# Two layers of a diffusion backbone: the gating and the second products of the expert passes, each moved a turn later

## The chip, the cores and the metric

One NeuronCore of one Trainium2 chip runs the whole program in one launch. The metric is the device time in microseconds (us), the median of several executions. Beside it stands one profiled execution, from which all rows below are taken. TensorE multiplies, VectorE, ScalarE and GpSimd work on elements, and SyncE issues the DMA transfers. Each engine runs its own instructions in order.

## The reference

Two layers work on 256 latent and 256 context tokens of width 1024. Layer 0 is a mixer of short convolution and attention, layer 1 a bidirectional RWKV-7 mixer, and each is followed by a PEER expert network: for each token and each of 8 heads the best 16 of 16384 single-neuron experts are chosen through product keys, and

```python
gate = jax.nn.softmax(top_s, axis=-1)
u = u_tab[idx]
v = v_tab[idx]
act = jax.nn.gelu(jnp.einsum('nd,nhkd->nhk', xc, u, preferred_element_type=jnp.float32), approximate=False)
return jnp.einsum('nhk,nhkd->nd', (gate * act).astype(v.dtype), v)
```

In layer 0 this network runs for the latent and for the context tokens, in layer 1 for the latent tokens only. All in float32.

## The kernel before

**The passes.** The expert network is not gathered but computed densely: a pass takes 256 tokens through all 16384 experts, in 128 blocks of 128 experts, one block E in each turn of the loop in `Peer.run` (L1166). A turn has these parts. `first(E)` (L1111) makes 24 matmuls of U with the tokens, 8 slices in three terms (high by high, low by high, high by low), into a PSUM tile H, and ScalarE applies GELU to H in place (L1120). `gate(E)` (L1123) multiplies H on VectorE with the block's gates G (L1127), zero for tokens that did not choose the expert, and splits the result into a high part `gwh` (ScalarE) and a low part `gwl` (VectorE). `second(E)` (L1133) makes 12 matmuls of 512 columns that add V times gates to four PSUM accumulators. `prep_u` and `prep_v` split the loaded U and V rows into high and low parts: `uh` and `vh` on ScalarE, `ul` half on VectorE and half on GpSimd, `vl` on GpSimd (on VectorE in every other turn of the first 32). `load_u` and `load_v` issue the 512 KB loads on the sync queue.

**The gates.** `gen(gq, j)` (L1019) prepares the gates of 32 blocks ahead, 16 tokens at a time, in every second turn: VectorE makes a one-hot `oh` of the low index, a one-hot `eq` of the high index and two products `A` of it with the gate's high and low part; 32 small matmuls (16 in layer 1) put them together in PSUM, and ScalarE copies them to G (in layer 1 VectorE adds the low parts).

**The order in a turn.** Source order in turn E: `first(E)`, `gate(E)`, `gen`, `second(E-1)`, `prep_v(E)`, load of V, `prep_u(E+1)`, `load_u(E+2)` and the store `keep_u`. At the turn between passes `second(E-1)`, the end of the pass and the split of the new tokens come first. The first 32 blocks of a `Peer` have their first products made ahead, so turns 0 to 31 have none. The tile framework places waits and may reorder instructions within an engine.

**Three passes.** The first `Peer` object runs two passes of layer 0 with the same U and V; in the first, low parts of U are stored to DRAM (`keep_u`) and in the second loaded back (`ul<-low`). The second `Peer` runs the pass of layer 1.

**The shadow.** Beside the two passes of layer 0 other work runs in four slots of every turn: the key scores and choices for the second pass, layer 1's modulation, and `rwkv_ctx` (L1999), the whole RWKV mixer of the context. These are generators that `beside` (L235) advances so that each is done on schedule: `rwkv_ctx` with NCTX = 530 units between turns 132 and 253. A `yield` names how many units the piece before it took. In its scan, `step` (L477) of one head pair makes a right side, its product (UV, copied by ScalarE and VectorE at L512), the state's update (L518) and pauses between them; `woven` sets the steps of one head pair beside the preparation of the next, with the factor `pace` on the pauses. The shadow's matmuls share four PSUM tiles (`mm`) with H and with the gates' products.

Of the kernel before, what the change touches and what calls it, by code (L numbers as in the profile page):

```python
# [253 lines left out]
class Scan:  # L254
# [222 lines left out]
    def step(self, i, S0, last=False):  # L477

        k, st, kn, pl = self.k, self.st, self.kn, self.ql
        V, S, T = k.V, k.S, k.T  # L480
        cs = (i, 3 - i)
        N = 128 * kn
        heads = [(d, j, hh, R2[hh]) for d in range(2) for j in range(kn) for hh in range(2)]

        def at(p, d, j, r):
            o = 64 * (kn * d + j)
            return p[r, o:o + 64]

        def f4(p):
            return p[:, :N].rearrange("p (d k n) -> p d k n", d=2, k=kn)  # L490

        def tile(name):
            return pl.tile([128, 2, kn, 64], F32, name=name, bufs=2 if name == "state" else None)

        rhs = self.ps()
        for d, j, hh, r in heads:
            T.matmul(at(rhs, d, j, r), lhsT=self.tri(d, hh, j, cs[d], 0)[self.fresh], rhs=self.UV[d][self.fresh, cs[d], j, hh],
                     start=d + j == 0, stop=S0 is None and d + j == kn)
        if S0 is not None:
            for d, j, hh, r in heads:  # L500
                T.matmul(at(rhs, d, j, r), lhsT=self.zop(d, hh, j, cs[d], 0), rhs=S0[r, d, j], start=False, stop=d + j == kn)
        yield from self.apart()
        rsb = self.right_side(f4(rhs))
        yield 0.5 if self.lean else None
        pu = self.ps()
        for d, j, hh, r in heads:
            T.matmul(at(pu, d, j, r), lhsT=self.rop(d, hh, 4 * j + cs[d]), rhs=rsb(d, hh, j), start=True, stop=True)
        yield from self.apart()
        for d in range(2):
            for hh in range(2):  # L510
                e = S.copy if hh == 0 else V.tensor_copy
                e(self.UV[d][R2[0], cs[d], :, hh], pu[R2[hh], 64 * kn * d:64 * kn * (d + 1)].rearrange("p (k n) -> p k n", k=kn))  # L512
        yield 0.5 if self.lean else None
        Sn = None
        if not last:
            pS = self.ps()
            for d, j, hh, r in heads:
                T.matmul(at(pS, d, j, r), lhsT=self.tok[d][:, j, cs[d], 64 * hh:64 * hh + 64], rhs=self.UV[d][:, cs[d], j, hh],  # L518
                         start=True, stop=True)
            yield from self.apart()  # L520
            Sn = tile("state")
            src = f4(pS)
            if S0 is not None:
                ts = Sn
                V.tensor_add(ts, S0, src)
                src = ts
            V.tensor_tensor(Sn, src, self.PC[:, i, :, :, None].to_broadcast([128, 2, kn, 64]), ALU.mult)
        if st:
            if i == 0:
                self.y = pl.tile([128, 4, kn, 64], F32, name="y", bufs=1)  # L530
            py = self.ps()
            for d, j, hh, r in heads:
                T.matmul(at(py, d, j, r), lhsT=self.zop(d, hh, j, cs[d], 1), rhs=S0[r, d, j], start=d + j == 0, stop=False)
            for d, j, hh, r in heads:
                T.matmul(at(py, d, j, r), lhsT=self.tri(d, hh, j, cs[d], 1), rhs=self.UV[d][:, cs[d], j, hh], start=False, stop=d + j == kn)
            y = self.y
            yi = (y[:, 0::3], y[:, 1:3], y[:, 2:0:-1], y[:, 3::-3])[i]
            if i < 2:
                S.copy(yi, f4(py))
            else:  # L540
                V.tensor_add(yi, yi, f4(py))
        yield 0.5 if self.lean else None
        return Sn

    def readout(self):
# [324 lines left out]
class Peer:  # L870
# [147 lines left out]

    def gen(self, gq, j):  # L1019

        n, q = divmod(gq, 4)
        pl, V = self.pl, self.k.V
        i16, g16 = self.IT[n]
# [14 lines left out]
        V.tensor_tensor(eq, self.iotaR[:, None, 32 * q:32 * q + 32].to_broadcast(sh), per_token(i16[:, 0]).to_broadcast(sh), ALU.is_equal)  # L1038
        for i in range(2):
            V.tensor_tensor(A[:, i], eq, per_token(g16[:, i]).to_broadcast(sh), ALU.mult)  # L1040
        G = self.GT[gq]
        if gq == 0 or self.shadow:
            p = self.k.mm() if gq else self.k.acc()
            for m in range(16):
# [16 lines left out]
    def load_u(self, E):  # L1061
        if E < self.NT:
            n, e = divmod(E, 128)
            ur = self.pu.tile([128, D], F32, name="raw", bufs=4)
            self.k.Y.dma_start(ur, self.k.I["peer_u"][self.passes[n][0], e])
            ul = None
            if self.again(n):
                ul = self.pu.tile([128, 8, 128], F32R, name="ul", bufs=2)
                self.k.Y.dma_start(ul.rearrange("p t i -> p (t i)").bitcast(F32), self.LOW[e])
            self.U[E] = ur, ul  # L1070

    def again(self, n):

# [49 lines left out]
    def gate(self, E):  # L1123
# [1 line left out]
        W = self.W[E]  # L1125
        W2 = self.k.mm()[:, :256] if E < LOOK else W
        self.k.V.tensor_mul(W2, W, self.GT[E // 32][:, E % 32])  # L1127
        wh = pl.tile([128, 256], F32R, name="gwh", bufs=2)
        wl = pl.tile([128, 256], F32R, name="gwl", bufs=2)
        self.k.split(wh, wl, W2)  # L1130
        self.W[E] = (wh, wl)

    def second(self, E, slot=lambda: None):  # L1133
# [11 lines left out]
                slot()  # L1145
        if e == 127:
            self.finish(n)

    def finish(self, n):
        k = self.k  # L1150
# [13 lines left out]
        self.load_v(E + 2)  # L1164

    def run(self):  # L1166
        NT, NP = self.NT, len(self.passes)
        self.load_v(1)
        for E in range(NT + 1):
            if E == LOOK:  # L1170
                self.ew.close()
            slot = (lambda: self.shadow(E)) if self.shadow and LOOK <= E < NT else (lambda: None)
            turn = E % 128 == 0 and 0 < E
            if E % 128 == 125:
                self.near(E // 128)
            if turn:
                self.last(E - 1, slot)
                if E < NT:
                    self.load_x(E // 128)
                self.en.close()  # L1180
            if LOOK <= E < NT:
                self.first(E, slot)
            if E < NT:
                self.gate(E)
                gq = E // 32 + 1
                if gq < 4 * NP and E % 2 == 0:
                    if gq % 4 == 0 and E % 32 == 0:
                        self.begin(gq // 4)
                    self.gen(gq, (E % 32) // 2)
            slot()  # L1190
            if E > 0 and not turn:
                self.last(E - 1, slot)
            else:
                slot()
            if LOOK <= E + 1 <= NT:
                self.prep_u(E + 1)
                if LOOK <= E:
                    self.load_u(E + 2)
            slot()
            if LOOK <= E + 1 < NT:  # L1200
                self.keep_u(E + 1, self.U[E + 1][1])
        self.es.close()
        self.er.close()


class K:
# [792 lines left out]
    def rwkv_ctx(self, hd, dr, sS, lean=True):  # L1999
# [3 lines left out]
        with tc.tile_pool(name="sU", bufs=1, reuse_waits="tile") as U, tc.tile_pool(name="sA", bufs=1, reuse_waits="tile") as A, tc.tile_pool(name="sP", bufs=1, reuse_waits="tile") as tp:  # L2003
# [37 lines left out]
            yield from prepare(0)  # L2041
            for g in range(8):
                yield from sc.rows()
                yield from woven(chunks(sc.twin(), g, 1.7 if g < 7 else 1.0), prepare(g + 1) if g < 7 else iter(()))

    def mixer1_tensors(self):
        dp = self.dp
# [236 lines left out]
```

## Time and profile before

| | us |
|---|---|
| median of 3 runs | 3877.7 |
| lowest and highest | 3869.63 and 3879.46 |
| the profiled execution | 3874.92 |
| its span, first to last instruction | 3873.1 |
| passes of layer 0, first second product to end | about 506 to 2483 |
| pass of layer 1, second products | about 3176 to 3867 |

Over the span TensorE is busy 90%, VectorE 65%, ScalarE 45%, GpSimd 46%, and the mean granted TensorE clock is 0.942. The layer 0 passes end in two places: the first at about 1394 us, the second at about 2483 us. Busy TensorE time includes matmuls at half clock, so busy time and granted clock are read together.

### The profile page before, as it was taken

How to read it: one execution, taken by the hardware profiler on the slowest of the kernel's cores; microseconds unless marked ns; L12 is line 12 of the kernel's file. 1: busy time of each engine (PE TensorE's matmuls, PEld its weight loads, DVE VectorE, ACT ScalarE, POOL GpSimd, SP SyncE). 2: the span in 40 equal slices, each digit the busy share in tenths (PEclk: the TensorE clock that was granted, in tenths of full speed). 3: DMA queues.
4: the chain of work that ended last, by engine and by line, in shares of the span. 5: the costliest groups of instructions: out<-in, count | busy, mean ns of one | idle time of the engine just before them, and what ended most of it. 6: DMA issues, size and time to landing. Idle time of an engine off the chain costs nothing.

```text
span 3873.1 us, 73036 instructions
## 1 busy us (share of the span) xinstructions
PE 3482.2 (90%) x29031; PEld 3035.8 (78%) x29031; DVE 2503.7 (65%) x5274; ACT 1726.0 (45%) x2815; POOL 1798.4 (46%) x1000
## 2 busy tenths in 40 slices
PE   7998889998899899998999999886787778999999
PEld 6678778997787688987877777785676776899998
DVE  3569897658954466446766655478877889655622
ACT  3343455554443355554444444453223344555544
POOL 1122545665454544443333333434434443677776
PEclk9999899999899999999999999897898889999999
DMA  7373656776588777764555555541024234555554
GB/s 241 113 241 130 213 175 216 256 244 214 193 298 287 255 275 250 249 220 169 189 186 180 190 200 186 179 150 25 17 73 136 90 108 142 169 179 180 178 186 155
DMA packets 337535, 710.51 MB, mean 183 GB/s; under 512 B 41220, under 2 KB 199560, under 8 KB 336168
## 3 DMA queue, kind: packets, MB, share of 16 engines
q1 hardware_dynamic: 337192, 705.84, 55.0%
q8 instruction: 227, 3.72, 0.4%
q14 instruction: 116, 0.95, 0.1%
HBM read 624.45 MB, written 81.30 MB: 182 GB/s over the span
## 4 chain that ended last, share of the span: by engine, by line
PE 35%; DVE 14%; issue 2%; POOL 2%; ACT 2%; DMA 0%; DVEq 0%; POOLq 0%; ACTq 0%; SPq 0%
PE acc L1142 12%; PE mm L1247 6%; PE mm L1248 5%; PE mm L1249 5%; DVE A L1040 1%; DVE prod L465 1%; PE mm L727 1%; DVE TT L468 1%; PE mm L851 1%; DVE oh L1034 1%; DVE zz L654 1%; DVE vl L1243 1%; DVE mm L1127 1%; DVE wz L841 0%; PE mm L518 0%
## 5 line engine op out<-in xcount | busy, mean ns | idle before, releaser
L1243 POOL TENSOR_TENSOR vl<-raw,vh 128x1024 fp32r<-128x1024 f32 x352 | 902.5, 2564 | 949.7 <-ACT vh L1242 893.0
L1247 PE MATMUL mm<-xh,uh 128*128 128x256 f32 x3072 | 899.6, 293 | 30.2 <-ACT uh L1096 29.7
L1248 PE MATMUL mm<-xh,ul 128*128 128x256 f32 x3072 | 891.5, 290 | 22.6 <-DVE ul L1101 16.1
L1249 PE MATMUL mm<-xl,uh 128*128 128x256 f32 x3072 | 885.5, 288 | 0.0
L1101 POOL TENSOR_TENSOR ul<-raw,uh 128x512 fp32r<-128x512 f32 x320 | 503.0, 1582 | 388.6 <-ACT uh L1096 358.5
L1247 PEld LDWEIGHTS mm<-xh,uh 128*128 128x128 f32 x3072 | 604.0, 197 | 56.5 <-ACT uh L1096 34.6
L1248 PEld LDWEIGHTS mm<-xh,ul 128*128 128x128 f32 x3072 | 605.2, 197 | 39.8 <-DVE ul L1101 20.8
L1249 PEld LDWEIGHTS mm<-xl,uh 128*128 128x128 f32 x3072 | 605.2, 197 | 16.2 <-issue 15.7
L1127 DVE TENSOR_TENSOR mm<-mm,G 128x256 f32<-128x256 f32 x320 | 137.1, 429 | 645.7 <-ACT mm L1120 645.0
L1142 PE MATMUL acc<-vh,gwh 128*128 128x512 f32 x1536 | 517.8, 418 | 39.6 <-ACT gwh L1242 37.0
L1242 ACT CAST vh<-raw 128x1024 fp32r<-128x1024 f32 x384 | 403.0, 1049 | 296.8 <-issue 167.2
L1142 PE MATMUL acc<-vh,gwl 128*128 128x512 f32 x1536 | 499.9, 407 | 17.2 <-DVE gwl L1243 16.0
L1142 PE MATMUL acc<-vl,gwh 128*128 128x512 f32 x1536 | 494.4, 403 | 13.4 <-DVE vl L1243 11.9
L1096 ACT CAST uh<-raw 128x1024 fp32r<-128x1024 f32 x384 | 400.1, 1042 | 14.5 <-DMA raw<-in_peer_u_dram 14.3
L1120 ACT ACTIVATE mm<-mm 128x256 f32<-128x256 f32 x320 | 117.9, 368 | 596.7 <-PE mm L1249 595.8
L1142 PEld LDWEIGHTS acc<-vh,gwl 128*128 128x128 f32 x1536 | 293.5, 194 | 98.8 <-DVE gwl L1243 34.5
L1142 PEld LDWEIGHTS acc<-vl,gwh 128*128 128x128 f32 x1536 | 296.7, 194 | 85.1 <-DVE vl L1243 15.1
L1142 PEld LDWEIGHTS acc<-vh,gwh 128*128 128x128 f32 x1536 | 268.2, 195 | 88.5 <-ACT gwh L1242 41.5
L1034 DVE TENSOR_TENSOR oh<-iotaR,i 128x2048 f16<-128x2048 f16 x192 | 268.4, 1398 | 19.6 <-ACT i L949 19.6
L1040 DVE TENSOR_TENSOR A<-eq,g 128x512 f16<-128x512 f16 x384 | 222.3, 610 | 53.2 <-PE mm L1047 25.0
L1101 DVE TENSOR_TENSOR ul<-raw,uh 128x512 fp32r<-128x512 f32 x192 | 192.9, 1005 | 61.4 <-ACT uh L1096 61.3
L1242 ACT CAST gwh<-mm 128x256 fp32r<-128x256 f32 x384 | 143.9, 375 | 173.0 <-DVE mm L1127 172.4
(421 smaller groups left out, 6148.0 us busy)
## 6 DMA issues: line engine op xcount, KB each, us to landing
raw<-in_peer_u_dram SPq DMA_DIRECT2D x384, 512.0 KB
raw<-in_peer_v_dram SPq DMA_DIRECT2D x384, 512.0 KB
low<-ul SPq DMA_DIRECT2D x128, 512.0 KB
ul<-low SPq DMA_DIRECT2D x128, 512.0 KB
wraw<-in_ada_w_dram SPq DMA_DIRECT2D x48, 1024.0 KB
wraw<-in_peer_wq_dram SPq DMA_DIRECT2D x16, 1024.0 KB
wraw<-in_ev_w_in_dram SPq DMA_DIRECT2D x9, 1024.0 KB
wraw<-in_ev_w_out_dram SPq DMA_DIRECT2D x8, 1024.0 KB
```

Source lines behind the costliest of these rows:

```text
L1034: V.tensor_tensor(oh, self.iotaR[:, None].to_broadcast([128, 8, 128, 2]), per_token(i16[:, 1]).to_broadcast([128, 8, 128, 2]), ALU.is_equal)
L1040: V.tensor_tensor(A[:, i], eq, per_token(g16[:, i]).to_broadcast(sh), ALU.mult)
L1096: k.S.copy(uh, ur)
L1101: (le or (k.V, k.P)[i]).tensor_sub(ul[:, t], ur[:, t], uh[:, t].bitcast(F32))
L1120: self.k.S.activation(W, H, AF.Gelu)
L1127: self.k.V.tensor_mul(W2, W, self.GT[E // 32][:, E % 32])
L1142: self.k.T.matmul(self.ACC[n][2 * tb + dh], lhsT=a[:, 128 * tb:128 * tb + 128], rhs=b[:, 512 * dh:512 * dh + 512], start=e == 0 and a is w ...
L1242: self.last_copy = self.S.copy(hi, src).ins
L1243: (le or self.V).tensor_sub(lo, src, hi.bitcast(F32))
L1247: self.T.matmul(out, lhsT=ah, rhs=bh, start=start, stop=False)
L1248: self.T.matmul(out, lhsT=al, rhs=bh, start=False, stop=False)
L1249: self.T.matmul(out, lhsT=ah, rhs=bl, start=False, stop=stop)
```

## The change

In `Peer.run`, turn E now begins with `gate(E-1)`, then loads the tokens at a turn between passes, prepares the low part of U for the next turn and issues the raw load of U for E+2, makes the one-hots (`spread`, the first half of `gen`), then `first(E)`, the load of a kept low part (`load_low`), then `second(E-2)` with `prep_v(E-1)` and the load of V, then the gates' products (`gather`, the second half of `gen`), and the store. The loop has two turns more. `gwh` and `gwl` get a third buffer. In the lean scan's `step` three pauses of 0.5 become 1.0, and the pace 1.7 becomes 1.4.

```diff
@@ Scan.step (three places)
-        yield 0.5 if self.lean else None
+        yield 1.0 if self.lean else None
@@ Peer.gen is cut in two
+        self.spread(gq, j)
+        self.gather(gq, j)
+    def spread(self, gq, j):
...
+        self.hot = oh, A
+    def gather(self, gq, j):
+        V, G, s, (oh, A) = self.k.V, self.GT[gq], slice(16 * j, 16 * j + 16), self.hot
@@ Peer.load_u
-            ul = None
-            if self.again(n):
-                ul = self.pu.tile([128, 8, 128], F32R, name="ul", bufs=2)
-                self.k.Y.dma_start(ul.rearrange("p t i -> p (t i)").bitcast(F32), self.LOW[e])
-            self.U[E] = ur, ul
+            self.U[E] = ur, None
+    def load_low(self, E):
+        n, e = divmod(E, 128)
+        if E < self.NT and self.again(n):
+            ul = self.pu.tile([128, 8, 128], F32R, name="ul", bufs=2)
+            self.k.Y.dma_start(ul.rearrange("p t i -> p (t i)").bitcast(F32), self.LOW[e])
+            self.U[E] = self.U[E][0], ul
@@ Peer.gate
-        wh = pl.tile([128, 256], F32R, name="gwh", bufs=2)
-        wl = pl.tile([128, 256], F32R, name="gwl", bufs=2)
+        wh = pl.tile([128, 256], F32R, name="gwh", bufs=3)
+        wl = pl.tile([128, 256], F32R, name="gwl", bufs=3)
@@ Peer.run, the loop after
+        for E in range(NT + 2):
+            slot = (lambda: self.shadow(E)) if self.shadow and LOOK <= E < NT else (lambda: None)
+            if 0 < E <= NT:
+                self.gate(E - 1)
             if E == LOOK:
                 self.ew.close()
+            if E < NT and E % 128 == 125:
                 self.near(E // 128)
+            if E < NT and E % 128 == 0 and E:
+                self.load_x(E // 128)
+            if LOOK <= E + 1 < NT:
                 self.prep_u(E + 1)
                 if LOOK <= E:
                     self.load_u(E + 2)
+            gq = E // 32 + 1
+            due = gq < 4 * NP and E % 2 == 0
+            if due:
+                if gq % 4 == 0 and E % 32 == 0:
+                    self.begin(gq // 4)
+                self.spread(gq, (E % 32) // 2)
+            if LOOK <= E < NT:
+                self.first(E, slot)
+                self.load_low(E + 2)
             slot()
+            if E > 1:
+                self.last(E - 2, slot)
+            if due:
+                self.gather(gq, (E % 32) // 2)
             if LOOK <= E + 1 < NT:
                 self.keep_u(E + 1, self.U[E + 1][1])
+            slot()
@@ rwkv_ctx
-                yield from woven(chunks(sc.twin(), g, 1.7 if g < 7 else 1.0), prepare(g + 1) if g < 7 else iter(()))
+                yield from woven(chunks(sc.twin(), g, 1.4 if g < 7 else 1.0), prepare(g + 1) if g < 7 else iter(()))
```

`finish`, which ends a pass, now also closes the pool of the pass's last rows (in `second`), as `run` did before.

## Rows read from the trace of the kernel before

**Rows 1.** By stage: stretch, length, busy PE, PEld, DVE, ACT, POOL; clock, DMA, GB/s
```profile
620.00:1000.00 380.00, 358.64 (x2967) 327.24 (x2962) 261.61 (x638) 184.99 (x269) 220.49 (x107) 0.97 0.71 236
1000.00:1390.00 390.00, 350.35 (x2875) 286.50 (x2875) 229.18 (x437) 165.06 (x252) 193.63 (x94) 0.96 0.77 264
1390.00:1800.00 410.00, 386.85 (x3281) 349.47 (x3281) 216.45 (x400) 210.34 (x345) 180.60 (x107) 0.97 0.70 238
1800.00:2483.00 683.00, 635.83 (x5625) 540.80 (x5624) 399.12 (x853) 306.69 (x532) 241.45 (x127) 0.95 0.56 188
3176.00:3300.00 124.00, 103.47 (x622) 77.43 (x621) 120.44 (x175) 57.19 (x95) 44.80 (x18) 0.94 0.41 136
3300.00:3865.00 565.00, 565.00 (x3991) 514.00 (x3991) 279.66 (x479) 286.61 (x448) 420.62 (x190) 1.00 0.55 176
```

**Rows 2.** Waits of TensorE, 620 to 2483 us: total us, times, longest
```profile
PE mm L518 <- DVE UV L512: 38.4, 21, 4.0
PE acc L1142 <- ACT gwh L1242: 30.8, 17, 3.8
PE mm L1248 <- DVE ul L1101: 16.1, 13, 4.6
PE acc L1142 <- DVE gwl L1243: 10.9, 11, 3.8
PE mm L667 <- DVE bk L633: 8.3, 4, 4.2
...
PE mm L518 <- ACT UV L512: 3.5, 5, 1.1
PE mm L1247 <- ACT uh L1096: 3.4, 4, 2.2
PE mm L1047 <- DVE A L1040: 3.2, 1, 3.2
PE acc L1142 <- ACT vh L1242: 2.6, 1, 2.6
```

**Rows 3.** Waits of TensorE, 1000 to 1390 us
```profile
PE mm L1248 <- DVE ul L1101: 15.4, 12, 4.6
```

**Rows 4.** Waits of VectorE and of ScalarE, 506 to 2483 us
```profile
DVE mm L1127 <- ACT mm L1120: 389.9, 117, 7.6
ACT gwh L1242 <- DVE mm L1127: 163.8, 76, 6.9
```

**Rows 5.** Busy time around one gap of TensorE, at the end of a pass
```profile
1384.00:1388.10 4.10, 1.52 (x7) 0.93 (x5) 2.92 (x5) 3.26 (x6) 0.00 (x0) 0.95 0.79 282
1388.10:1394.30 6.20, 5.81 (x13) 4.13 (x14) 2.87 (x4) 2.09 (x2) 3.64 (x2) 0.50 0.97 363
1394.30:1403.80 9.50, 9.50 (x94) 8.95 (x93) 6.66 (x11) 4.74 (x8) 4.48 (x3) 0.99 0.85 306
```

**Rows 6.** Timeline of one turn, VectorE and GpSimd: start us, length us, engine, line
```profile
3607.37 1.20 DVE L1034 TENSOR_TENSOR oh<-iotaR,i 128x2048 f16<-128x2048 f16 x1
3608.50 2.62 DVE L1038 TENSOR_TENSOR eq<-iotaR,i 128x512 f16<-128x512 f16 x1
...
3611.39 1.52 DVE L1101 TENSOR_TENSOR ul<-raw,uh 128x512 fp32r<-128x512 f32 x1
...
3607.52 3.33 POOL L1243 TENSOR_TENSOR vl<-raw,vh 128x1024 fp32r<-128x1024 f32 x1 [0.53 <-DVE G L1059]
```

**Rows 7.** Timeline of VectorE in one step of the scan
```profile
2113.83 0.23 DVE L512 COPY UV<-mm 64x64 f32<-64x64 f32 x1
2113.97 1.03 DVE L474 STREAM_TRANSPOSE X<-TT 128x512 f32<-128x512 f32 x1
...
2115.52 0.19 DVE L512 COPY UV<-mm 64x64 f32<-64x64 f32 x1
```

**Rows 8.** Timeline of ScalarE in one turn
```profile
1492.19 1.03 ACT L1096 CAST uh<-raw 128x1024 fp32r<-128x1024 f32 x1
...
1494.33 0.37 ACT L1242 CAST gwh<-mm 128x256 fp32r<-128x256 f32 x1
```

More of the change, by code (lines that the diff above doesn't have):

```diff
@@ L512, in step @@
                 e(self.UV[d][R2[0], cs[d], :, hh], pu[R2[hh], 64 * kn * d:64 * kn * (d + 1)].rearrange("p (k n) -> p k n", k=kn))
-        yield 0.5 if self.lean else None
+        yield 1.0 if self.lean else None
         Sn = None
@@ L541, in step @@
                 V.tensor_add(yi, yi, f4(py))
-        yield 0.5 if self.lean else None
+        yield 1.0 if self.lean else None
         return Sn
@@ L1040, in gen @@
             V.tensor_tensor(A[:, i], eq, per_token(g16[:, i]).to_broadcast(sh), ALU.mult)
-        G = self.GT[gq]
+        self.hot = oh, A
+    def gather(self, gq, j):
+        V, G, s, (oh, A) = self.k.V, self.GT[gq], slice(16 * j, 16 * j + 16), self.hot
         if gq == 0 or self.shadow:
@@ L1147, in second @@
             self.finish(n)
+            self.en.close()
     def finish(self, n):
@@ L1168, in run @@
         self.load_v(1)
-        for E in range(NT + 1):
+        for E in range(NT + 2):
+            slot = (lambda: self.shadow(E)) if self.shadow and LOOK <= E < NT else (lambda: None)
+            if 0 < E <= NT:
+                self.gate(E - 1)
             if E == LOOK:
                 self.ew.close()
-            slot = (lambda: self.shadow(E)) if self.shadow and LOOK <= E < NT else (lambda: None)
-            turn = E % 128 == 0 and 0 < E
-            if E % 128 == 125:
+            if E < NT and E % 128 == 125:
                 self.near(E // 128)
[L1176 to L1195, printed above, removed]
+            if E < NT and E % 128 == 0 and E:
+                self.load_x(E // 128)
+            if LOOK <= E + 1 < NT:
                 self.prep_u(E + 1)
```

## The prediction

> **What bounds the kernel now.** I read the stages first: one row of busy time for each stretch, cut where the turns change character [rows 1]. A turn handles one block E of 128 experts: 24 first products, a GELU, a gating, 12 second products. From 3300 to 3865 us TensorE is busy for 565.00 of 565 us at granted clock 1.00: 96 turns of 5.9 us with no gap, so no reordering can shorten them. From 3176 to 3300 us (turns 0 to 31 of the last pass, which have no first products) VectorE is busy 120.44 of 124 us and sets the pace. The two passes of layer 0 are the open part. In the four stretches from 620 to 2483 us TensorE is idle for 21.4 + 39.6 + 23.1 + 47.2 = 131.3 us, while no other engine is over 70% busy; there the turns also carry shadow work of other stages.
>
> Second, who ended these idle times [rows 2]. The rows shown make 117.2 of the 131.3 us: second products waiting for gates or V parts (gwh 30.8, gwl 10.9, vh 2.6, together 44.3), first products waiting for U parts (ul 16.1, uh 3.4, together 19.5, of which 15.4 lie between 1000 and 1390 us [rows 3]), gates' products waiting for A (3.2), and 41.9 us in a shadow, the scan's state product L518 waiting for its UV copies. That last wait is nearly all of the idle time after 1800 us.
>
> Third, why the gates are late [rows 4]. VectorE stood still 389.9 us, 117 times, in front of the gating product L1127 because the GELU of the same turn was not done, 3.3 us each time, with everything behind it on VectorE standing too; ScalarE stood 163.8 us in front of gwh for that same product. Gate and second product are links of a chain inside one turn.
>
> Fourth, the price of a gap beyond its own length [rows 5]. From 1384.0 to 1388.1 us TensorE worked 1.52 us of 4.1. The 13 matmuls behind it ran at granted clock 0.50 and filled 6.2 us; then 0.99 came back. The gap cost about as much again as it lasted. A granted clock of 0.97, 0.96, 0.97 and 0.95 in the four stretches [rows 1], taken as work lost, is 11.4 + 15.6 + 12.3 + 34.2 = 73.5 us.
>
> **The gating, a turn later.** gate(E-1) opens turn E: one VectorE product, one ScalarE copy, one VectorE subtraction, none new. Its GELU ended a turn earlier, so VectorE no longer stops for it, and the second products that need these gates come in turn E+1, over 5 us on. All of the 44.3 us has its cause removed; what was queued behind the blocked product (one-hots, low parts, the shadow's copies) is freed also. A wait on ScalarE stays: the GELU still sits in its queue and waits for TensorE, with shadow copies behind it.
>
> **The low part and load of U.** prep_u(E+1) (uh on ScalarE, halves of ul on VectorE and GpSimd) moves from the end of turn E to its head, so first(E+1) has a whole turn of cover. 19.5 us is open to this. On the sync queue the load of raw for E+2 moves to the head with it, before the V load and before what the shadow issues; its lead to its cast stays one turn. The load of a kept low part now comes behind first(E), which frees its buffer, and is needed in turn E+2. The store of a low part stays at the end, when it has long been ready, so it stops holding the queue. If cover is gone anywhere, it is DMA: between 1000 and 1390 us the engines are 0.77 busy, and in the gap rows 0.79 and 0.97 [rows 1, 5]. A transfer that is late stays late, so I cut the first three classes (44.3 + 19.5 + 3.2 = 67) by a quarter: 50 us gained, bounds 30 and 67.
>
> **One-hots first, gates' products last.** No instruction is added: four VectorE operations go to the head, 32 (later 16) small matmuls and the copy to the end. The 3.2 us for A is counted above. What this adds: in every second turn the head holds gating, a low half, oh, eq and two A in one block of VectorE. Its operations stretch beside GpSimd: eq took 2.62 us at 3608.50 while GpSimd's vl ran for 3.33 us from 3607.52 [rows 6]. oh, eq and a low half make 1.20 + 2.62 + 1.52 = 5.3 us in these rows; with gating and A I estimate the block at 4 us where nothing stretches and 8 where all does. The shadow's VectorE copies of the first slot stand behind it. Also the first product now sits in its PSUM buffer (one of four shared with the shadow) until the next turn's gating rather than for a few us. The trace of before has neither state. Nearest row: the shadow waits that are not for gates, bk with 8.3 us [rows 2]; and the UV class with 41.9 us is what such queueing costs when it is bad. I charge 30 us with their clock, nearer to the small class; bounds 0 and 85, the two classes doubled by half again for the clock.
>
> The Trainium skill, "SBUF — State Buffer", section "SBUF: two separate sides", says that VectorE and GpSimd share one port pair as a lock, the loser standing for the other's whole instruction. The eq row agrees: it ended at 3611.1 with vl's end at 3610.9. By that rule the head's one-hots would meet only a low half on GpSimd instead of vl, and in the pass with kept low parts nothing; the charge would be near 0 and the sum 107 us, 3768 us, which lies on the side of rival (a).
>
> **Shadow steps.** The lean scan's three pauses of 0.5 become 1.0 and the pace 1.7 becomes 1.4. The space between the UV copies and L518 goes from 0.85 to 1.4 units, where a slot gets 530/(4 x 121) = 1.1 units; so the two never share a slot. Not all is cured: at 2113.83 and 2115.52 us the two halves of a UV copy are parted by a transpose of 1.03 us and another in VectorE's own queue [rows 7]. I take half, 20 us; bounds 0 and 42. The length: per head group 4 x 4.5 x 1.7 = 30.6 units become 4 x 6 x 1.4 = 33.6, both below the 37.5 units of the preparation woven beside it, so only the last group grows, 18 to 24 units of 530, some 1.4 turns, hidden while the scan still ends before turn 253 (my count is about 522 of 530).
>
> **Clock.** Before 1800 us the gained 50 is 60% of the 84 us idle, and I take 60% of 39.3: 23 us. After it 20 of 47.2 us goes: 42% of 34.2, 14 us. Bounds 0 and 73.
>
> **Ends and edges.** Two turns more in the loop, without work of their own; the second products are the same number. At the turn between passes the x split now stands straight before first(128) and the old gap [rows 5] goes: 0, bounds -6 and +6. Turns 0 to 31 are VectorE's: 0, bounds -4 and +4 [rows 1]. The deeper gwh and gwl buffers cost nothing in time.
>
> **Sum.** 50 + 20 + 23 + 14 - 30 = 77, say 75 us, against the profiled execution of 3874.9 us (1.8 us around its span): 3800 us. The median of the runs, 3877.7, lies 2.8 us above that execution; I do not correct for it.
>
> **The rivals.** (a) More comes back: the classes go whole, 67 + 42, with their share of the clock (109/131 of 73.5, 61), less 30: 3735 us. For it: gaps and slow clock go together in the rows. (b) The shadow takes most of it: TensorE runs in order, shorter turns leave the shadow's copies less time, and UV-like waits grow. Gates gain 50 + 23, no gain in the scan, charge 50: about 3850 us. (c) The order in the text is not the order on the engines: at 1492.19 us ScalarE ran uh, which the text puts last in the turn, ahead of gwh at 1494.33 us [rows 8]; if the builder already sorts by readiness, little moves: 3875 us. Against it: 389.9 us of blocked gating product shows that the sorting does not reach over turns. (d) Slower: the block at the turn's head. With 96 one-hot turns in the shadowed part, the 107 us of gains are used up when TensorE waits 1.1 us longer in each; at 1.4 us it is 134 us, 27 us over: 3902 us. For it: a block of 4 to 8 us, against some 1.5 us between two slots (5.9 us by four). Against it: before, the same block stood in the middle of the turn, with a 3.3 us stop in front of it [rows 4].
>
> **How the numbers follow.** Forecast (3770 to 3830) 0.48; (a) 0.17; (b) 0.16; (c) 0.08; (d) 0.11. A measurement of this kernel tells about 0.3%, 12 us, from no change. Forecast, (a) and (b) are faster: 0.81; (c) is the same: 0.08; (d) is slower: 0.11. The range leaves out (d), most of (c) and the far end of (a): 3725 to 3870.
>
> **What the profile after would show.** L1127 no longer waits for L1120; L1142 hardly waits for gwh and gwl, L1248 not for ul; TensorE's idle time from 620 to the end of layer 0's passes near 75 us and the granted clock there near 0.98; the two passes some 75 us shorter in all; L518's waits about halved. The last 96 turns stay 565 us. The forecast is wrong if new waits of shadow matmuls for VectorE or for a PSUM buffer come in their place, or if V or U casts wait for DMA between 1000 and 1390 us.

## The result and the profile after

The changed kernel takes 3811.79 us (median; 3805.39 to 3815.91), the kernel before 3875.26 us in the same session: a ratio of 0.9842, with a 95% interval from 0.9823 to 0.9861, or 63.5 us less. The forecast was 3800 us. Its profiled execution took 3805.39 us, 69.5 us less than that of before.

To see where these 69.5 us lie I cut both traces at the first matmul of the same blocks, so that a stretch is the same work in every kernel. Blocks 0 to 127 are the first pass of layer 0, 128 to 255 the second, 256 to 383 the pass of layer 1. Each row below is the difference of two start times in one profiled execution, in us. Beside before and after stand the four runs that answer most; they come below.

| from first product to first product | before | after | e1 order only | e2 steps only | e7 low part last | e8 gating in turn |
|---|---|---|---|---|---|---|
| start to block 32 (with turns 0–31) | 616.3 | 610.9 | 615.7 | 614.6 | 611.8 | 615.2 |
| 32 to 64 | 254.7 | 252.0 | 256.6 | 254.1 | 252.8 | 253.7 |
| 64 to 96 | 249.7 | 250.7 | 249.4 | 247.8 | 250.5 | 248.9 |
| 96 to 127 | 259.0 | 233.7 | 232.9 | 259.9 | 264.7 | 233.9 |
| 127 to 132, end of a pass | 37.6 | 44.5 | 42.4 | 37.9 | 39.3 | 44.1 |
| 132 to 160 | 231.6 | 230.7 | 230.4 | 231.7 | 228.1 | 232.2 |
| 160 to 255, the scan beside it | 825.9 | 798.3 | 807.5 | 800.5 | 808.3 | 806.5 |
| layer 1's mixer, to block 287 | 699.1 | 696.3 | 696.0 | 693.7 | 696.3 | 695.9 |
| 287 to 288: turns 0–31, last pass | 130.7 | 115.0 | 115.8 | 130.6 | 116.0 | 127.6 |
| 288 to the last second product | 561.2 | 564.4 | 564.4 | 561.2 | 564.4 | 561.6 |

Three rows carry the gain: 25.3, 27.6 and 15.7 us. One row costs: the end of the pass, 6.9 us. The mixer row, where the kernels do not differ, scatters from 693.7 to 702.3 us over all runs below, so a difference of some 8 us in one row of one profile proves little by itself.

The stages of the kernel after; the columns are those of [rows 1].

```profile
620.00:1000.00 380.00, 360.10 (x3012) 326.71 (x3011) 266.01 (x670) 189.64 (x271) 217.80 (x107) 0.98 0.71 237
1000.00:1390.00 390.00, 360.58 (x3046) 300.47 (x3045) 227.17 (x424) 172.69 (x264) 202.56 (x98) 0.96 0.81 283
1390.00:1800.00 410.00, 387.06 (x3321) 348.60 (x3320) 246.76 (x422) 218.13 (x355) 186.78 (x108) 0.97 0.69 230
1800.00:2431.00 631.00, 593.06 (x5396) 509.92 (x5395) 393.55 (x809) 292.42 (x508) 233.33 (x120) 0.97 0.58 198
3117.00:3232.00 115.00, 100.48 (x643) 77.81 (x641) 112.44 (x175) 60.00 (x100) 47.63 (x19) 0.96 0.46 152
3232.00:3786.00 554.00, 554.00 (x3936) 499.66 (x3937) 291.15 (x478) 285.60 (x444) 382.62 (x188) 1.00 0.55 179
```

In the first four rows TensorE is idle 19.9 + 29.4 + 22.9 + 37.9 = 110 us, where it was 131.3; the clock's share, worked out as in the prediction, is 7.6 + 15.6 + 12.3 + 18.9 = 54 us, where it was 73.5. The last row is full at clock 1.00 as before.

TensorE's waits after, 620 to 2431 us: total us, times, longest. They answer to [rows 2].

```profile
PE mm L1260 <- DVE ul L1112: 24.1, 15, 3.1
PE mm L518 <- DVE UV L512: 13.6, 14, 2.3
PE mm L501 <- DVE state L527: 11.3, 5, 3.6
...
PE mm L507 <- DVE rsb L742: 4.6, 2, 2.3
PE mm L727 <- DVE R L720: 4.6, 5, 1.9
PE mm L727 <- DVE t L697: 4.3, 1, 4.3
```

The waits for `gwh` and `gwl` (30.8 and 10.9 us) are gone. `ul` (L1112, L1101 before) is now the largest with 24.1 us. Of the shadow's waits, L507 and L727 are new, and L501 has grown from 1.0 us. All but 0.6 us of the waits for `ul` lie between blocks 64 and 96 (862.8 to 1113.5 us):

```profile
PE mm L1260 <- DVE ul L1112: 23.5, 14, 3.1
```

### The profile page after: what moved, and what is told of

It is laid out like the page before. It is cut to its first block, busy times and chain, and to the rows that moved or that the text cites. A ratio compares the mean times of both kernels' runs of the same rounds, so it can differ in the third digit from the quotient of the medians.

```text
span 3803.6 us, 73097 instructions
## 1 busy us (share of the span) xinstructions
PE 3438.2 (90%) x29031; PEld 3003.0 (79%) x29031; DVE 2532.4 (67%) x5274; ACT 1737.4 (46%) x2817; POOL 1772.1 (47%) x1000
## 5 line engine op out<-in xcount | busy, mean ns | idle before, releaser
L1255 POOL TENSOR_TENSOR vl<-raw,vh 128x1024 fp32r<-128x1024 f32 x352 | 879.5, 2499 | 856.8 <-ACT vh L1254 776.4
L1259 PE MATMUL mm<-xh,uh 128*128 128x256 f32 x3072 | 909.2, 296 | 36.0 <-ACT uh L1107 32.6
L1260 PE MATMUL mm<-xh,ul 128*128 128x256 f32 x3072 | 897.4, 292 | 36.8 <-DVE ul L1112 24.1
L1112 POOL TENSOR_TENSOR ul<-raw,uh 128x512 fp32r<-128x512 f32 x320 | 497.5, 1565 | 484.6 <-ACT uh L1107 433.4
L1153 PE MATMUL acc<-vh,gwh 128*128 128x512 f32 x1536 | 503.1, 408 | 11.2 <-ACT gwh L1254 9.1
L1153 PE MATMUL acc<-vh,gwl 128*128 128x512 f32 x1536 | 485.9, 397 | 4.8 <-DVE gwl L1255 4.5
L1153 PE MATMUL acc<-vl,gwh 128*128 128x512 f32 x1536 | 483.6, 396 | 4.2 <-POOL vl L1255 4.1
L1045 DVE TENSOR_TENSOR A<-eq,g 128x512 f16<-128x512 f16 x384 | 331.7, 890 | 116.5 <-PE mm L1055 64.7
L1153 PEld LDWEIGHTS acc<-vh,gwh 128*128 128x128 f32 x1536 | 264.8, 192 | 56.2 <-ACT gwh L1254 10.9
L1039 DVE TENSOR_TENSOR oh<-iotaR,i 128x2048 f16<-128x2048 f16 x192 | 254.3, 1324 | 21.6 <-ACT i L949 19.5
L1112 DVE TENSOR_TENSOR ul<-raw,uh 128x512 fp32r<-128x512 f32 x192 | 186.3, 970 | 86.6 <-ACT uh L1107 86.4
```

The source lines that it names most:

```text
L1039: V.tensor_tensor(oh, self.iotaR[:, None].to_broadcast([128, 8, 128, 2]), per_token(i16[:, 1]).to_broadcast([128, 8, 128, 2]), ALU.is_equal)
L1112: (le or (k.V, k.P)[i]).tensor_sub(ul[:, t], ur[:, t], uh[:, t].bitcast(F32))
L1153: self.k.T.matmul(self.ACC[n][2 * tb + dh], lhsT=a[:, 128 * tb:128 * tb + 128], rhs=b[:, 512 * dh:512 * dh + 512], start=e == 0 and a is w ...
L1255: (le or self.V).tensor_sub(lo, src, hi.bitcast(F32))
L1259: self.T.matmul(out, lhsT=ah, rhs=bh, start=start, stop=False)
L1260: self.T.matmul(out, lhsT=al, rhs=bh, start=False, stop=False)
```

## Experiments

Theory: the reordering gains because the links inside a turn (gating before second product, low part before first product) lose their waits; the steps gain in the scan. Rivals: one of the two does it all; and in turns 0 to 31 the cause is the meeting of VectorE and GpSimd.

**Order and steps apart (e1, e2).** e1 is the kernel after with the old steps, e2 the kernel before with the new ones. The edit of e1, which stands in three places of `step` for the first line (that of e2 is its reverse on the kernel before):

```diff
-        yield 1.0 if self.lean else None
+        yield 0.5 if self.lean else None
...
-                yield from woven(chunks(sc.twin(), g, 1.4 if g < 7 else 1.0), prepare(g + 1) if g < 7 else iter(()))
+                yield from woven(chunks(sc.twin(), g, 1.7 if g < 7 else 1.0), prepare(g + 1) if g < 7 else iter(()))
```

> The changed kernel with the scan's old pauses (0.5) and pace (1.7): the new order of the turn alone. Read: the time from the first product of turn 160 to that of turn 255, 826.0 us before and 798.2 us with the whole change. Theory 'order': VectorE freed from the blocked gating makes the scan's copies earlier; the stretch stays at some 800 us and the whole at some 3815 us. Rival 'steps': the space between UV copy and state product does it; the stretch goes back to some 820 us or more and the whole to some 3835 us, and TensorE's waits of L518 for UV are back near 40 us.

> The kernel before with the scan's new pauses (1.0) and pace (1.4) and nothing else. Theory 'steps': turns 160 to 255 take some 800 us instead of 826, L518's waits for UV fall from 42 to some 15 us, the whole is some 3850 us. Rival 'order': the stretch stays within 5 us of 826, the whole within 8 us of 3875.

Measured: e1 3825.25 us, 0.9888 [0.9871, 0.9904]; e2 3845.54 us, 0.9939 [0.9922, 0.9956]. The gains in turns 96 to 127 and in turns 0 to 31 of the last pass belong to the order: e1 has them, e2 does not. In the scan the order alone gives 18.4 us and the steps alone 25.4, both together 27.6. L518's waits for the VectorE copy are 38.4 us before, 27.3 in e1, 21.7 in e2 and 13.6 after. So these waits fall by 11.1 and 16.7 us and nearly add up, to 24.8, while the lengths do not: other waits come in their place, L501 with the steps (7.7 us in e2, 11.3 after) and L507 and L727 with the order (16.7 us in e1). Both theories had a part; neither alone described the scan.

**Whose turn makes `vl` (e3, e4).** In turns 0 to 31 VectorE makes `vl` in the odd turns and GpSimd in the even ones. The one-hots come in the even turns. After the change `prep_v` runs a turn later than before, so GpSimd's `vl` falls into turns without one-hots. e3 gives that arrangement to the kernel before, e4 takes it from the kernel after; the line is the same in both:

```diff
-        self.k.split(vh, vl, vr, self.k.V if E < LOOK and E % 2 else self.k.P)
+        self.k.split(vh, vl, vr, self.k.V if E < LOOK and E % 2 == 0 else self.k.P)
```

> The kernel before; in turns 0 to 31 the V low part goes to VectorE in even turns (those with one-hots) and to GpSimd in odd ones, the other way round than before. The change had this effect unasked, as the V part comes a turn later there. Theory 'collision': VectorE's operations lose time beside a GpSimd operation, and GpSimd's 2.7 us low part now stands beside a gating only; turns 0 to 31 of the last pass go from 130.7 to some 117 us, the whole to some 3858 us. Rival 'gating': the new order of gating made those turns shorter; they stay at 131 us within 3 us and the whole at 3875 us.

> The changed kernel with the same swap, which puts GpSimd's V low part beside the one-hots again. Theory 'collision': turns 0 to 31 of the last pass go from 115.0 back to some 129 us, the whole from some 3812 to some 3828 us. Rival 'gating': they stay at 115 us within 3 us.

Measured: e3 3868.2 us, 0.9997 [0.9986, 1.0007]; e4 3823.7 us, 0.9876 [0.9859, 0.9892]. In the stretch of block 287 to 288 e4 lost 10.7 us of the 15.7 (125.7), near what the collision theory said, but e3 gained only 2.4 (128.3) where some 14 were expected. VectorE's groups in this stretch show both (line, operation, tiles, count | busy us, mean ns | idle before). Before:

```profile
L1243 DVE TENSOR_TENSOR vl<-raw,vh 128x1024 fp32r<-128x1024 f32 x16 | 29.3, 1830 | 0.5 <-ACT vh L1242 0.5
L1034 DVE TENSOR_TENSOR oh<-iotaR,i 128x2048 f16<-128x2048 f16 x17 | 22.9, 1344 | 0.0
L1040 DVE TENSOR_TENSOR A<-eq,g 128x512 f16<-128x512 f16 x33 | 20.8, 642 | 2.8 <-PE mm L1054 2.8
L1127 DVE TENSOR_TENSOR mm<-W,G 128x256 f32<-128x256 f32 x32 | 18.4, 583 | 0.0
```

After:

```profile
L1138 DVE TENSOR_TENSOR mm<-W,G 128x256 f32<-128x256 f32 x32 | 26.5, 871 | 0.0
L1039 DVE TENSOR_TENSOR oh<-iotaR,i 128x2048 f16<-128x2048 f16 x16 | 19.4, 1215 | 0.0
L1255 DVE TENSOR_TENSOR vl<-raw,vh 128x1024 fp32r<-128x1024 f32 x15 | 18.2, 1215 | 0.0
L1045 DVE TENSOR_TENSOR A<-eq,g 128x512 f16<-128x512 f16 x32 | 14.6, 495 | 0.1
```

e4, where `A` now meets GpSimd, and e8 (below), where `oh` and `A` do:

```profile
L1045 DVE TENSOR_TENSOR A<-eq,g 128x512 f16<-128x512 f16 x31 | 38.1, 1267 | 0.0
```

```profile
L1039 DVE TENSOR_TENSOR oh<-iotaR,i 128x2048 f16<-128x2048 f16 x16 | 36.3, 2271 | 0.0
L1045 DVE TENSOR_TENSOR A<-eq,g 128x512 f16<-128x512 f16 x31 | 27.1, 908 | 0.0
```

And e3's timeline (start, length), two meetings with the undisturbed operations of the next turns:

```profile
3207.80 4.00 POOL L1243 TENSOR_TENSOR vl<-raw,vh 128x1024 fp32r<-128x1024 f32 x1 [7.34 <-ACT vh L1242]
...
3209.79 2.29 DVE L1038 TENSOR_TENSOR eq<-iotaR,i 128x512 f16<-128x512 f16 x1
...
3214.72 2.41 POOL L1243 TENSOR_TENSOR vl<-raw,vh 128x1024 fp32r<-128x1024 f32 x1 [2.92 <-ACT vh L1242]
3215.08 2.34 DVE L1127 TENSOR_TENSOR mm<-W,G 128x256 f32<-128x256 f32 x1
...
3219.48 0.41 DVE L1038 TENSOR_TENSOR eq<-iotaR,i 128x512 f16<-128x512 f16 x1
3219.81 0.42 DVE L1127 TENSOR_TENSOR mm<-W,G 128x256 f32<-128x256 f32 x1
```

`eq` takes 0.41 us alone and 2.29 beside `vl`, the gating product 0.42 and 2.34. Which operation pays, the order decides: in e3 the meeting only moved on to `eq` and to the product. I added up, for VectorE's operations of this stretch that ran beside GpSimd, the time that each took beyond the shortest of its kind in the same trace: 31.2 us before, 36.0 in e3, 22.6 after, 32.6 in e4 and 36.7 in e8. From after to e4 this sum grows by 10.0 us and the stretch by 10.7. So the meeting is the main mechanism, the kernel after has cheaper meetings, and the rule "odd or even" by itself does not give that. It is not all: between before and after it accounts for 8.6 of the 15.7 us, and in e3 the sum grew by 4.8 us while the stretch lost 2.4. What makes the rest was not followed.

**The end of the pass (e5).** In the kernel after, ScalarE waits for the new tokens and later a store holds the sync queue. Timeline:

```profile
1355.97 2.18 ACT L1254 CAST xh<-xT 128x512 fp32r<-128x512 f32 x4 [4.38 <-DMA xT<-xD]
...
1374.76 5.33 SPq L1170 DMA_DIRECT2D hD<-h  x4
```

Busy time in and behind TensorE's two gaps (columns of [rows 5]):

```profile
1353.07:1359.15 6.08, 0.01 (x2) 0.00 (x1) 2.50 (x4) 3.13 (x5) 0.00 (x0) 0.93 1.01 412
1359.15:1364.70 5.55, 5.55 (x25) 5.55 (x26) 0.00 (x0) 1.08 (x2) 2.37 (x1) 0.50 0.83 299
1383.62:1385.72 2.10, 0.00 (x1) 0.01 (x1) 0.00 (x0) 1.05 (x1) 0.00 (x0) 0.98 0.97 298
1385.72:1392.00 6.28, 5.91 (x14) 4.23 (x15) 0.86 (x2) 3.79 (x5) 3.87 (x2) 0.50 1.02 401
```

There are two gaps where [rows 5] had one, and behind each the granted clock is 0.50, the lower of the two levels (1.2 of 2.4 GHz). e5 loads the tokens first and issues the stores at the end of the following turn, 130:

```diff
@@ near
+        if n + 1 < len(self.passes):
+            self.xT = pool.tile([128, 8, 256], F32, name="xT")
+            Y.dma_start(self.xT, self.passes[n + 1][2])
...
-        if n + 1 < len(self.passes):
-            self.xT = pool.tile([128, 8, 256], F32, name="xT")
-            Y.dma_start(self.xT, self.passes[n + 1][2])
@@ finish
-                k.Y.dma_start(hd[:, tb, cs], h)
+                self.stores.append((hd[:, tb, cs], h))
@@ run
+            if E % 128 == 2 and E > 128:
+                for o, h in self.stores:
+                    self.k.Y.dma_start(o, h)
+                self.en.close()
```

> The changed kernel with two edits at the turn between passes: the new tokens xT are loaded first in near(), ahead of the rows and gate vectors, and the four stores of the finished rows are issued at the end of turn 130 instead of right in the finish, so that they don't hold the sync queue while the sums are made. Read: first product of turn 127 to that of turn 132, 37.6 us before the change and 44.5 after. Theory: the change put the split of xT straight before the first products (a gap of 6.1 us until xT landed, then half clock) and the waiting stores hold the V load (a gap of 2.1 us, then half clock); the stretch falls to some 33 us, the whole by some 10 us to 3802 us. Rival: the V and U loads are late because the DMA engines are full there; the stretch stays over 41 us.

Measured: the stretch fell from 44.5 to 38.3 us; a gap of 4.46 us and one of 1.29 us are left. That is between the theory's 33 us and the rival's 41, and no shorter than before the change (37.6). The kernel takes 3811.62 us, 0.9829 [0.9804, 0.9853]: 6 us in one place cannot be told from the kernel after by its total.

**Low part and gating apart (e7, e8).** e7 is the kernel after with the preparation and the loads of U, both together, taken from ahead of the one-hots back to the end of the turn; e8 is the kernel after with the gating back in its own turn, behind `first(E)`, and the second products one turn later, as before:

```diff
@@ e7
-            if LOOK <= E + 1 < NT:
-                self.prep_u(E + 1)
-                if LOOK <= E:
-                    self.load_u(E + 2)
...
             if LOOK <= E + 1 < NT:
+                self.prep_u(E + 1)
+                if LOOK <= E:
+                    self.load_u(E + 2)
+                    self.load_low(E + 2)
                 self.keep_u(E + 1, self.U[E + 1][1])
@@ e8
-            if 0 < E <= NT:
-                self.gate(E - 1)
...
+            if E < NT:
+                self.gate(E)
-            if E > 1:
-                self.last(E - 2, slot)
+            if E > 0:
+                self.last(E - 1, slot)
```

> The changed kernel with the low part of U, its load and the load of kept low parts back at the end of the turn; gating, one-hots and second products stay a turn later. Read: turns 96 to 127, 259.0 us before and 233.7 us after. Theory 'low part': U's cover of a turn gave this gain; waits for ul are back and the stretch goes to 245 us or more, the whole to some 3825 us. Rival 'gating': VectorE freed from the blocked gating is what brings ul in time; the stretch stays under 239 us and the whole within 8 us of 3812.

> The changed kernel with gating again behind the first products of its own turn and the second products one turn later instead of two; low part and one-hots first and gates' products last stay. Theory 'gating': the blocked gating product is back (some 390 us of VectorE standing, against 265), second products wait for gwh and gwl again in turns 64 to 127 (some 30 us), the whole some 3840 us. Rival 'low part': the earlier low part and one-hots carry the gain; the whole stays within 8 us of 3812.

Measured: e7 3847.15 us, 0.9936 [0.9919, 0.9952]; e8 3832.31 us, 0.9898 [0.9882, 0.9915]. The 25 us of turns 96 to 127 hang on what e7 takes back (264.7, in e8 233.9). The gain in turns 0 to 31 of the last pass goes with e8's edit (127.6, in e7 116.0). But e8 takes the V part back by a turn together with the second products, so GpSimd's `vl` stands beside the one-hots again, as in e4; that the gating itself gave this gain is not shown. In the scan each is worth 8 to 10 us. In the first pass, where the trace of before showed the waits for gates, the gating's place is worth nothing that shows. Between blocks 64 and 96 of e8 the waits for gates are back, those for `ul` are gone, and the length is 248.9 us where it was 250.7:

```profile
PE acc L1153 <- ACT gwh L1254: 21.8, 11, 4.9
```

The expectation for e8 missed in one point: VectorE's stop in front of the gating product did not go back to some 390 us; it is 272.0 us (615 to 2434 us), and 283.5 in e7. So the gating's place is not what shortened it.

**What in the low part's place (e9, e10, e11).** Turns 96 to 127 of four kernels, one row each: before, after, e7 and e10.

```profile
1120.70:1379.70 259.00, 234.23 (x2006) 187.15 (x2005) 131.42 (x187) 103.63 (x162) 125.70 (x62) 0.98 0.79 273
```

```profile
1113.50:1347.20 233.70, 225.75 (x2006) 184.18 (x2005) 118.18 (x183) 102.97 (x160) 127.32 (x62) 0.99 0.85 294
```

```profile
1115.10:1379.80 264.70, 236.75 (x2006) 190.03 (x2005) 133.63 (x184) 104.03 (x161) 125.59 (x62) 0.95 0.76 266
```

```profile
1118.30:1373.10 254.80, 233.94 (x2007) 188.00 (x2006) 132.91 (x184) 103.37 (x160) 123.00 (x62) 0.97 0.82 277
```

DMA share times length is 205, 199, 201 and 209 us: the transfers are busy about as long in each, and stand idle 54, 35, 64 and 46 us. I suspected the store `keep_u`, which waits for `ul` at the head of the sync queue with raw loads behind it. Waits of the sync queue, 1120 to 1360 us, before, after and e10:

```profile
SPq L1081 <- DVE ul L1101: 138.9, 25, 10.9
```

```profile
SPq L1092 <- DVE ul L1112: 63.4, 24, 11.0
```

```profile
SPq L1073 <- POOL vl L1261: 122.8, 25, 9.5
```

Three kernels issue the store a turn later, when `ul` has long been there: e9 on e7, e10 on e5, e11 on before. The new lines stand behind the second products, and `ulow` is the low part that `first(E)` uses.

```diff
-                self.keep_u(E + 1, self.U[E + 1][1])
...
+            if LOOK <= E < NT:
+                self.keep_u(E, self.ulow)
```

> The kernel after with the low part of U at the end of the turn (as in e7), and the store of the low part (keep_u) a turn later, behind the second products, when that part has long been ready. Compared with e7, in the stretch from the first product of block 96 to that of block 127 (264.7 us in e7, 233.7 in the kernel after). Theory A, the store that waits for ul at the head of the sync queue holds back the raw loads behind it: the hold of the store, 139.2 us in these turns in e7, nearly goes, the stretch falls to 236 to 242 us, and the kernel to about 3823 us. Theory B, the part itself is late, with too little cover between the cast and the product: the hold goes but the stretch stays at 260 to 265 us, the waits of first products for ul stay at about 16 us, and the kernel stays at about 3847 us.

> The kernel after with the earlier token load and later stores at the end of a pass (as in e5) and the store of the low part a turn later. By theory A the rest of the hold in the kernel after (63.4 us in turns 96 to 127) goes too and the raw loads come earlier; the stretch of turns 96 to 127 can lose at most a few us of its 233.7, say 230, and the kernel comes to about 3805 us. By theory B nothing changes against e5: 233.6 us and about 3811 us.

> The kernel before with one change: the store of the low part comes a turn later, behind the second products. By theory A the hold of the store, 141.1 us in turns 96 to 127, nearly goes and the stretch falls from 259.0 to 236 to 242 us, the kernel from 3873 to about 3852 us. By theory B the stretch stays at 255 to 259 us, the first products still wait some 15 us for ul between 1000 and 1390 us, and the kernel stays within 5 us of 3873.

Measured: e9 3843.56 us, 0.9937 [0.9917, 0.9957], stretch 254.2; e10 3834.05, 0.9906 [0.9888, 0.9923], stretch 254.8; e11 3885.22, 1.0041 [1.0027, 1.0055], stretch 273.1. Theory A falls. The store's hold did shrink (58.1 us in e9, 57.0 in e11), and only e9 gained, 10 us of 31; on the two others the stretch grew by 21 and 14 us, and no length that either theory named came out. The hold went to other issues: in e10 the raw load L1073 stands 122.8 us, by the profile for GpSimd's `vl`.

e10 is no test of theory B, though the text of its program has the early low part, for on the engines it is not early. The cast and VectorE's half of the low part for block 108, and the gating product of block 107, after and in e10:

```profile
1201.68 1.08 ACT L1107 CAST uh<-raw 128x1024 fp32r<-128x1024 f32 x1
1202.94 1.79 DVE L1112 TENSOR_TENSOR ul<-raw,uh 128x512 fp32r<-128x512 f32 x1
1204.66 0.42 DVE L1138 TENSOR_TENSOR mm<-mm,G 128x256 f32<-128x256 f32 x1
```

```profile
1206.93 1.08 ACT L1107 CAST uh<-raw 128x1024 fp32r<-128x1024 f32 x1
1211.09 0.43 DVE L1138 TENSOR_TENSOR mm<-mm,G 128x256 f32<-128x256 f32 x1 [0.39 <-ACT mm L1131]
1212.30 0.68 DVE L1112 TENSOR_TENSOR ul<-raw,uh 128x512 fp32r<-128x512 f32 x1
```

In 28 of 31 turns after, VectorE's half stands ahead of the gating of the block before; in e10 it stands behind it in 26. In the median of blocks 97 to 127 it is ready 6.3 us ahead of its block's first product after, 1.0 us before, 0.6 in e7, 0.1 in e9, 0.3 in e11, and 0.7 in e10. In e10 the cast is as early as after (7.7 and 7.3 us ahead), so raw load and cast alone do not give the gain. In all fourteen kernels the two go together: where this lead is 6.3 us the stretch takes 233 to 234 us, where it is 1.0 or less at least 254. So the gain of this stretch goes with the low part early on the engines, as theory B has it. What the store's place adds, and why the builder orders e10 otherwise, stays open.

**The turns that gained nothing, 64 to 96 (e6, e12).** Here the shadow makes the choices of the second pass, and VectorE is full. Before, and after:

```profile
930.00:990.00 60.00, 52.28 (x407) 45.15 (x405) 60.00 (x243) 24.62 (x36) 31.18 (x15) 0.91 0.62 209
990.00:1050.00 60.00, 49.37 (x344) 42.16 (x344) 60.00 (x230) 26.87 (x37) 28.41 (x14) 0.86 0.54 181
```

```profile
920.00:980.00 60.00, 48.55 (x387) 42.49 (x386) 60.00 (x232) 23.83 (x34) 29.18 (x16) 0.94 0.61 203
980.00:1040.00 60.00, 47.80 (x335) 41.81 (x334) 59.76 (x242) 27.55 (x38) 24.75 (x14) 0.89 0.55 187
```

e6 spreads these choices over more turns, e12 moves VectorE's half of the low part to GpSimd, which is idle more than half of these 120 us:

```diff
@@ e6
-WKEYS, WPAIR, WPROJ = 2.2, 2.2, 1.7
+WKEYS, WPAIR, WPROJ = 3.2, 3.2, 1.7
@@ e12
-                self.prep_u(E + 1)
+                self.prep_u(E + 1, self.k.P if 64 <= E < 96 else None)
```

> The changed kernel with the units of the shadow's key choices (VectorE work) raised from 2.2 to 3.2, so that the same work spreads over some 32 turns instead of 26, and the score products are pressed into fewer turns. Turns 64 to 96 took 249.7 us before and 250.7 us after the change, and VectorE is busy 60.0 of 60 us in two thirds of a minute-long part of it (920 to 1040 us). Theory: VectorE is the bound there, so a thinner stream of VectorE work lets turns 32 to 96 (502.6 us) end some 10 to 15 us earlier, TensorE's waits for ul there (23.5 us) fall by half; the whole some 3800 us. Rival: the waits come from the order or from PSUM buffers; turns 32 to 96 stay within 4 us of 502.6.

> The kernel after, with the low part of U of turns 64 to 95 made by GpSimd alone (VectorE's half moves to it). In the kernel after VectorE is busy 60.00 of 60 us from 920 to 980 us and 59.76 of 60 from 980 to 1040, and its halves of ul take 11.7 us of these 120; GpSimd is busy there for 54 of 120 us. Theory A, a full VectorE sets the length of these turns: the stretch from the first product of block 64 to that of block 96 falls from 250.7 to 238 to 244 us, and TensorE's waits for VectorE's ul there go. Rival, VectorE is full only because it always has shadow work to fill with, and the links between turns set the length: the stretch stays at 249 to 253 us, with waits for GpSimd's ul in place of VectorE's. The kernel comes to about 3802 us by theory A and stays at 3812 by the rival.

Measured: e6 3810.61 us, 0.9847 [0.9828, 0.9865]: turns 64 to 96 took 243.3 us, 7.4 less, but 32 to 64 took 11.3 more. Together that is 3.9 us more, within the rival's bounds, and the waits for `ul` hardly fell (21.9 us from 23.5); but VectorE was still full there, so a thinner stream was not reached. e12 3824.49 us, 0.988 [0.9864, 0.9897]: the stretch took 259.8 us, 9.1 more, which neither theory had, and VectorE was as full as ever:

```profile
920.00:980.00 60.00, 45.25 (x333) 36.48 (x331) 59.97 (x224) 23.72 (x34) 33.07 (x20) 0.97 0.52 177
```

Over the whole stretch `ul` gave back 27.8 us of VectorE, yet its busy time was 213.2 us where it had been 216.4: with the same counts `eq` rose from 694 to 1243 ns, `A` from 967 to 1057, the candidates' operation from 269 to 356, beside a GpSimd that was busy 170 instead of 128 us. TensorE now waited 25.7 us for `vl` and `vh`. So e12 did not lighten VectorE and cannot tell whether a lighter one would shorten these turns. That a full VectorE sets them is read from the rows; e8 shows only that there one wait replaces another at nearly the same length.

## Why the prediction was right or wrong

The total was near, the mechanism of the low part and of the scan right in kind. But part of the total came from a place priced at nothing, and the largest term, the gates, gave nothing in the first pass, so that the total came so near is in part luck.

- **Gates, 44.3 us of waits, cut to three quarters.** Wrong in its effect. The waits for `gwh` and `gwl` went, and in the first pass nothing was gained by that (e8: 253.7 + 248.9 + 233.9 us for blocks 32 to 127, after 252.0 + 250.7 + 233.7). The step that failed is the step from waits to time. "No other engine is over 70% busy" was a mean over 380 us and hid 120 us with VectorE at 100%. There TensorE only changed the name of its wait: 26.4 us for gates (`gwh`, `gwl`) in e8 and 24.7 before, 23.5 for `ul` after, between blocks 64 and 96.
- **VectorE no longer stops for the GELU.** Wrong. It stood 389.9 us [rows 4] and still stands 269.1 (620 to 2431 us), now in front of the gating of the block before:

```profile
DVE mm L1138 <- ACT mm L1131: 269.1, 96, 11.4
```

  Even what fell is not the gating's: with the gating back in its own turn it stood 272.0 us (e8). What shortened it was not separated. Where VectorE has time to spare it reaches the gating early, and the GELU is still the last link. The stop is much the same in e8 and after, and e8 is some 20 us slower: it was no measure of the gain.
- **Low part, 19.5 us of waits.** Right mechanism and right place (1000 to 1390 us, [rows 3]), undersized: 25.3 us in turns 96 to 127 alone. TensorE's busy time there fell too, 234.23 to 225.75 us for the same 2006 matmuls, part of it the clock (0.98 to 0.99). The prediction said that the store stops holding the queue; the hold was halved, but e9 and e11 show that the hold by itself is not the price. e7 puts the place of preparation and raw load at 31 us in these turns, and e10, with the cast early and the low part late, points to the low part.
- **Scan, 20 of 41.9 us.** Right in kind: L518's waits for the two copies fell by 28.3 us. But the order alone shortens the scan by 18.4 us and the steps alone by 25.4 (e1, e2); I gave it to the steps alone.
- **Charge of 30 us for the block at the turn's head.** Right in kind. The shadow waits L501, L507 and L727 make 24.8 us where `bk` had 8.3, though L501 comes with the steps (e2). The upper bound of 85 us does not come out of its rows: 8.3 and 41.9 make 50.2, and half as much again 75. From the lock of the Trainium skill ("SBUF — State Buffer", section "SBUF: two separate sides") the prediction worked out a charge near 0, since the one-hots would no longer meet `vl`. The rows agree with the lock (2.29 against 0.41 us), not with that conclusion. Between blocks 32 and 128 the time that `oh`, `eq` and `A` took beyond the shortest of their kind is 71.6 us before and 78.5 after: `eq` fell from 36.1 to 7.5, `A` rose from 16.7 to 61.8, in 28 of 37 stretched cases beside `vl`.
- **Clock, 37 us.** Oversized: 19 us came back, since the idle time fell by 21 us and not by 56.
- **Turns 0 to 31: 0 within 4.** Wrong in the last pass: 15.7 us gained. VectorE was rightly named as its limit [rows 1], but I took its time as fixed by the number of operations. `vl`, `oh` and `A` took 73.0 us before and 52.2 after (some 3 us of it because one operation fewer of each fell into the window), the gating product 8.1 more: `vl` came a turn later with the second products, and that changed what meets GpSimd. e4 puts 10.7 us on this. [rows 6] showed the price; I did not ask which operations would pay it after the move.
- **End of the pass: 0 within 6.** Just outside: 6.9 us slower. The gap of [rows 5] did not go, it became two.
- **Rivals.** (b) is refuted by the 27.6 us gained in the scan; its idea, that the shadow takes the gain, fits turns 64 to 96. (a) described nothing. (c) is refuted by e1, though its ground, that the order in the text is not the order on the engines, shows in e10. (d) is refuted by the total.

In sum, blocks 32 to 255 gained 48.6 us where 75 were forecast. The rest of the 69.5 us is turns 0 to 31 of the last pass (15.7), what lies before block 32 (5.4) and the mixer row (2.8), less 3.2 us at the end, where one more block's second products now follow the last first product.

## What to carry to other kernels

Before pricing a wait, cut the trace into stretches short enough that an engine at 100% shows, and ask there what is late next: where VectorE was full, the wait changed its name and not its length. When an operation of VectorE or GpSimd is moved by a turn, list what runs on the other of the two at its old and at its new place; in 32 turns that was worth 10.7 us (e4). Before a run is taken as a test of an order, read that order on the engines from its trace; e10 did not have the one its text has. Cut before and after at the same work, not at the same times, and undo the parts one by one: gains of parts overlap and do not add.

## What was not expected of the hardware

A small operation can take five times its length beside GpSimd (`eq` 0.41 to 2.29 us, the gating product 0.42 to 2.34), and moving 27.8 us of work from VectorE to a half idle GpSimd freed 3.3 us of VectorE, because the rest of its work stretched (e12). After gaps of 6.08 and 2.10 us the granted clock was 0.50 for 5.55 and 6.28 us: the shorter gap cost no less than the longer one in slow time. And more than halving the time that a store held the sync queue did not shorten the kernel before: the hold fell from 138.9 to 57.0 us, the ratio is 1.0041 (e11), and other issues then held the queue.
